# A two-layer decoder trunk: the four weight-block sums of each seven-product pair are issued on GpSimd instead of VectorE

## The chip, the cores and the metric

The kernel runs on one core of a Trainium2 chip. The metric is the device time of one execution in microseconds (us), as a median over runs. In the profile's rows PE is TensorE's matmuls and PEld its weight loads, DVE is VectorE, ACT is ScalarE, POOL is GpSimd, and SPq is the queue of SyncE, which here only issues transfers.

## The reference

The trunk has two layers on 512 tokens of width 1024. Each layer runs a feed-forward block, a token mixer (latent attention in layer 0, sparse attention with shared keys and values in layer 1, each with four memory heads beside it) and a second feed-forward block, each followed by a layer norm. Only the four feed-forward blocks matter here:

```python
def swiglu(x, w_gu, w_down):
    g, u = jnp.split(x @ w_gu, 2, axis=-1)
    return (jax.nn.silu(g) * u) @ w_down
x = layer_norm(DN_ALPHA * x + 0.5 * swiglu(x, ffn_w_gu[layer, 0], ffn_w_down[layer, 0]), ...)
```

Here `w_gu` is 1024 x 5632, so each block has 22 column blocks of 128 for g and 22 for u, and `w_down` is 2816 x 1024.

## The kernel before, in words

**Precision.** Every operand is kept as two fp32r tiles, a rounded part `hi` and a remainder `lo`, and a product is three matmuls: hi·hi, hi·lo, lo·hi. Weights are read from HBM as f32 tiles of 128 x 1024 (`wraw`, a pool of 5 buffers, loaded on SP's queue by `load`, line 143). `split` makes the two parts: ScalarE casts the raw tile to `whi` (L216), VectorE writes `wlo` = raw − hi (L217), which has two inputs in SBUF. A pair `whi`, `wlo` lives in a ring of three, with four more inside the feed-forward blocks; it comes free when TensorE has read it for the last time.

**Seven products instead of eight.** In a feed-forward block, column block m of g and of u is computed for two halves of the tokens (columns 0 to 255 and 256 to 511), and the contraction over 1024 rows is cut in two halves of 512. That is a 2 x 2 by 2 x 2 product of blocks, and for 77 of the 88 column blocks (items "d" of the table `GROUPS`) it is done with seven block products. They need sums of token blocks, made once for each feed-forward block (`token_forms`, L427), and four sums of weight blocks for each pair (`combined`), with raw tiles g and u and a third one, d:

- L159: d(upper half) = g(lower) − u(lower)
- L160: u(lower) = u(lower) + u(upper)
- L165: d(lower) = u(lower) − g(lower)
- L168: g(upper) = g(upper) − d(lower)

Each is 128 x 512 f32 with both inputs in SBUF, and each reads what one before it wrote. The weight units of a pair are g0 (the raw g), g2 (the tile d), g1 (the tile u) and g3 (the upper half of g). `prep` makes unit after unit in the order of a list (`_unit_order`), up to four units ahead of the one that TensorE is to use.

**One pair on TensorE.** `sevens` runs for each pair j the products p6 and p7 (with d), the first half of the next pair (`m1`, with its g0), p5 and p4 (with u), the second half `m2` of the next pair, and p3 (with g3). Each of the seven is a `quarter`: 12 matmuls of 256 columns into half a PSUM bank. Between them stand short steps of other engines on PSUM banks: ScalarE copies a started bank into a new one (`seeded`, L590) and p7's result to SBUF (L613), VectorE adds p5's result to it (L618) and p4's (L622), both with one input in PSUM, and ScalarE applies silu (L603, L627). p5 accumulates into bank r2, L618 reads r2, and p3 accumulates on into the same r2: so p3 can start only when L618 has read the bank. Between p5 and p3 TensorE has p4 and `m2`. `finish` (L631, then a split to `hhi`, `hlo`) makes the input of the down projection.

**Groups.** The 22 column blocks are done in five groups of four or five. After each group the down projection adds its part for all four token tiles (L449 to L454, six matmuls of 512 columns each), and VectorE adds the result to the residual (L341, one input in PSUM). The first group of a block begins with two or three column blocks without the seven products (L643, L644).

**What sets the order.** The instructions of each engine run in the order in which the scheduler of the tile framework put them; each waits by semaphores for its inputs and buffers, and everything behind a waiting instruction on its engine waits too. The sums stand in VectorE's queue between the remainders of weight tiles (L217) and the steps on PSUM banks. GpSimd has, in the feed-forward blocks, two small transfers at the start (`apart`, L723) and four scalar powers in the norm at the end (L354); its other work lies in the attention.

Of the kernel before, what the change touches and what calls it, by code (L numbers as in the profile page):

```python
# [117 lines left out]
def tile_trunk(ctx: ExitStack, tc, a: dict, out):  # L118
    nc = tc.nc
# [21 lines left out]
    def load(src, n=1024):  # L141
        raw = wraw.tile([P, 1024], F32, name="wraw")
        nc.sync.dma_start(raw[:, :n], src[:, :n])
        return raw

    def combined(name, idx):


        l, f, m = idx
        lo, up = slice(0, 512), slice(512, 1024)  # L150
        op = nc.vector.tensor_tensor
        if name == "g0":
            W.pairs[idx] = [load(a["gu"][l, f, m, 0])]
            return W.pairs[idx][0]
        raws = W.pairs[idx]
        if len(raws) == 1:
            g, u, d = raws[0], load(a["gu"][l, f, m, 1]), wraw.tile([P, 1024], F32, name="wraw")
            raws += [u, d]
            op(d[:, up], g[:, lo], u[:, lo], op=ALU.subtract)  # L159
            op(u[:, lo], u[:, lo], u[:, up], op=ALU.add)  # L160
        g, u, d = raws
        if name == "g1":
            return u
        if name == "g2":
            op(d[:, lo], u[:, lo], g[:, lo], op=ALU.subtract)  # L165
            return d
        del W.pairs[idx]
        op(g[:, up], g[:, up], d[:, lo], op=ALU.subtract)  # L168
        return g[:, up]
# [9 lines left out]
    def prep():  # L179
        name, idx, n, scope = order[W.done]  # L180
        if name in ("g0", "g1", "g2", "g3"):
            raw = combined(name, idx)
            n = 512 if name == "g3" else n
        else:
            src = a[name]
            for i in idx:
                src = src[i]
            raw = load(src, n)
        hi, lo = ring(scope)
        split(hi[:, :n], lo[:, :n], raw[:, :n])  # L190
        W.ready[W.done] = (hi, lo)
        W.done += 1
# [1506 lines left out]
```

## Time and profile before

| | |
|---|---|
| time, median of 3 runs | 1850.78 us (1848.37 to 1850.85) |
| time of the profiled execution | 1853.04 us |
| its span | 1851.3 us |
| granted TensorE clock | 0.996 |

The profiled execution is 2.26 us above the median, and 1.74 us of its time lie outside the span. In the rows below, a group of instructions has its line, engine, operation and tiles (out <- in) with sizes in partitions x elements, then the count, the busy time in us and the mean of one in ns, then the idle time of the engine just before these instructions and what ended it. In a timeline the first column is the start in us, the second the duration in us; "x2" marks neighbours that were merged.

### The profile page before, as it was taken

The numbers are of one execution on the slowest core, as the hardware profiler recorded it, in microseconds if no ns is written. First come the engines' busy times: TensorE is split into PE (matmuls) and PEld (weight loads), VectorE is DVE, ScalarE is ACT, GpSimd is POOL, SyncE is SP. The second block draws the span as 40 slices with busy tenths as digits, with TensorE's granted clock in tenths as the row PEclk, the third lists the DMA queues.
The fourth block names the chain that finished last, engine by engine and source line by source line (L and its number), as shares of the span: only waits on it lengthen the run. The fifth ranks groups of instructions, "written<-read, shape, count | busy, mean of one in ns | idle before, by whom it ended". The sixth has DMA issues, their size and how long they took to land.

```text
span 1851.3 us, 31666 instructions
## 1 busy us (share of the span) xinstructions
PE 1831.2 (99%) x12753; PEld 1650.7 (89%) x12753; DVE 1346.2 (73%) x1979; ACT 914.9 (49%) x1671; POOL 170.3 (9%) x216
## 2 busy tenths in 40 slices
PE   9999999999999999999999999999999999999998
PEld 8899899996789999999999999999956699999997
DVE  8677777758678678677886876877667477677776
ACT  6345445456545345345653543544476354534542
POOL 0000000125500000000100000001266100000000
PEclk9999999999999999999999999999999999999999
DMA  7333235531134234224333323335321323323421
GB/s 259 103 126 111 97 112 162 181 107 35 58 112 156 70 102 149 69 92 160 123 120 115 125 83 112 115 121 171 107 56 21 124 71 120 114 82 112 132 75 69
DMA packets 60900, 204.90 MB, mean 111 GB/s; under 512 B 7152, under 2 KB 8320, under 8 KB 60752
## 3 DMA queue, kind: packets, MB, share of 16 engines
q1 hardware_dynamic: 57568, 194.46, 32.0%
q0 software_dynamic: 2752, 8.01, 1.3%
q8 instruction: 100, 1.64, 0.4%
q14 instruction: 48, 0.39, 0.1%
q10 hardware_dynamic: 432, 0.39, 0.1%
HBM read 188.16 MB, written 7.34 MB: 106 GB/s over the span
## 4 chain that ended last, share of the span: by engine, by line
PE 92%; DVE 4%; ACT 2%; issue 1%; DMA 1%; POOL 1%; POOLq 0%; DVEq 0%; ACTq 0%
PE bank L411 13%; PE bank L413 13%; PE bank L417 13%; PE bank L450 5%; PE bank L449 5%; PE bank L452 5%; PE bank L451 5%; PE bank L453 5%; PE bank L454 5%; PE bank L399 3%; PE bank L397 3%; PE bank L402 3%; PE tb L799 3%; PE o L827 2%; PE bank L386 2%; PE bank L384 2%
## 5 line engine op out<-in xcount | busy, mean ns | idle before, releaser
L216 ACT CAST whi<-wraw 128x1024 fp32r<-128x1024 f32 (+2 forms) x475 | 460.4, 977 | 534.2 <-PE bank L454 263.2
L217 DVE TENSOR_TENSOR wlo<-wraw,whi 128x1024 fp32r<-128x1024 f32 (+2 forms) x475 | 533.4, 1133 | 200.0 <-ACT whi L216 192.8
L411 PE MATMUL bank<-t,whi 128*128 128x256 f32 x1212 | 291.9, 277 | 0.0
L413 PE MATMUL bank<-t,whi 128*128 128x256 f32 x1212 | 291.6, 277 | 0.0
L413 PEld LDWEIGHTS bank<-t,whi 128*128 128x128 f32 x1212 | 227.8, 188 | 0.6
L411 PEld LDWEIGHTS bank<-t,whi 128*128 128x128 f32 x1212 | 227.7, 188 | 0.7
L411 PE MATMUL bank<-xhi,whi 128*128 128x256 f32 x924 | 223.0, 278 | 0.1
L413 PE MATMUL bank<-xlo,whi 128*128 128x256 f32 x924 | 222.2, 277 | 0.0
L417 PE MATMUL bank<-t,wlo 128*128 128x256 f32 x1232 | 190.6, 277 | 0.0
L411 PEld LDWEIGHTS bank<-xhi,whi 128*128 128x128 f32 x924 | 173.6, 188 | 2.4 <-DVE us L618 0.9
L413 PEld LDWEIGHTS bank<-xlo,whi 128*128 128x128 f32 x924 | 173.7, 188 | 1.2
L417 PEld LDWEIGHTS bank<-t,wlo 128*128 128x128 f32 x1232 | 163.3, 188 | 0.0
L341 DVE SCALAR_TENSOR_TENSOR x<-x,bank 128x512 f32<-128x512 f32 x176 | 112.2, 683 | 53.9 <-PE bank L453 51.7
L417 PE MATMUL bank<-xhi,wlo 128*128 128x256 f32 x924 | 143.1, 277 | 0.0
L354 POOL TENSOR_TENSOR st<-st,cst 128x1 f32<-128x1 f32 x24 | 15.8, 659 | 1368.0 <-DVE st L353 1343.1
L449 PE MATMUL bank<-whi,hhi 128*128 128x512 f32 x336 | 131.0, 390 | 0.0
L450 PE MATMUL bank<-whi,hhi 128*128 128x512 f32 x336 | 130.9, 390 | 0.0
L451 PE MATMUL bank<-wlo,hhi 128*128 128x512 f32 x336 | 130.8, 389 | 0.0
L454 PE MATMUL bank<-whi,hlo 128*128 128x512 f32 x336 | 130.7, 389 | 0.0
L452 PE MATMUL bank<-wlo,hhi 128*128 128x512 f32 x336 | 130.7, 389 | 0.0
L453 PE MATMUL bank<-whi,hlo 128*128 128x512 f32 x336 | 130.7, 389 | 0.0
L399 PE MATMUL bank<-xlo,whi 128*128 128x256 f32 x520 | 125.2, 281 | 2.3 <-DVE xlo L217 2.3
(340 smaller groups left out, 3592.1 us busy)
## 6 DMA issues: line engine op xcount, KB each, us to landing
wraw<-in_gu SPq DMA_DIRECT2D x173, 512.0 KB, 3.8
wraw<-in_dn SPq DMA_DIRECT2D x88, 512.0 KB, 4.1
wraw<-in_wo SPq DMA_DIRECT2D x16, 512.0 KB, 3.4
wraw<-in_wm SPq DMA_DIRECT2D x8, 512.0 KB, 4.3
x_dram<-x SPq DMA_DIRECT2D x8, 512.0 KB, 3.0
x<-x_dram SPq DMA_DIRECT2D x8, 512.0 KB, 4.4
wraw<-in_w SPq DMA_DIRECT2D x8, 512.0 KB, 3.4
wraw<-in_wq SPq DMA_DIRECT2D x6, 512.0 KB, 4.3
```

The costliest lines, as they stand in the source:

```text
L216: nc.scalar.copy(hi, src)
L217: return eng.tensor_tensor(lo, src, hi.bitcast(F32), op=ALU.subtract).ins
L399: nc.tensor.matmul(ps[:, c0:c1], lhsT=hi[:, k * P:(k + 1) * P], rhs=F.xlo[:, k, c0:c1], start=False, stop=False)
L411: nc.tensor.matmul(ps, lhsT=hi[:, ks], rhs=(xh if k else fh)[:, k], start=start and k == 0, stop=False, skip_group_check=True)
L413: nc.tensor.matmul(ps, lhsT=hi[:, ks], rhs=(xl if k else fl)[:, k], start=False, stop=False, skip_group_check=True)
L417: nc.tensor.matmul(ps, lhsT=lo[:, ks], rhs=xh[:, k], start=False, stop=k == 3, skip_group_check=True)
L449: nc.tensor.matmul(p0, lhsT=ahi, rhs=hi[:, 0:512], start=first, stop=False)
L450: nc.tensor.matmul(p1, lhsT=ahi, rhs=hi[:, 512:1024], start=first, stop=False)
L451: nc.tensor.matmul(p0, lhsT=ahi, rhs=lo[:, 0:512], start=False, stop=False)
L452: nc.tensor.matmul(p1, lhsT=ahi, rhs=lo[:, 512:1024], start=False, stop=False)
L453: nc.tensor.matmul(p0, lhsT=alo, rhs=hi[:, 0:512], start=False, stop=last)
L454: nc.tensor.matmul(p1, lhsT=alo, rhs=hi[:, 512:1024], start=False, stop=last)
```

## The change

The four sums of each pair are issued on GpSimd. Nothing else in the source changes; tiles, buffers and the list of units are the same.

```diff
@@ combined
         lo, up = slice(0, 512), slice(512, 1024)
-        op = nc.vector.tensor_tensor
+        op = nc.gpsimd.tensor_tensor
```

308 instructions (4 in each of 77 pairs) leave VectorE's queue and enter GpSimd's. TensorE's and SyncE's queues stay as they were. On the two others, some neighbours change places too, because the scheduler reckons with other ends.

The first place is a pair in the middle of a group of the first feed-forward block: sums into tile `wraw_3384`, between the L622 of one pair and the L618 of the next. VectorE before:

```order
L622 TENSOR_TENSOR us_3117<-us_3117,bank_3154 128x256
L217 TENSOR_TENSOR wlo_3298<-wraw_3295,whi_3297 128x1024
L217 TENSOR_TENSOR wlo_3264<-wraw_3259,whi_3263 128x1024
L159 TENSOR_TENSOR wraw_3384<-wraw_3295,wraw_3382 128x512
L631 SCALAR_TENSOR_TENSOR sg_3168<-sg_3168,us_3117 128x512
L217 TENSOR_TENSOR wlo_3317<-wraw_3257,whi_3316 128x1024
L217 TENSOR_TENSOR hlo_3116<-sg_3168,hhi_3115 128x512
L217 TENSOR_TENSOR wlo_3362<-wraw_3170,whi_3361 128x512
L160 TENSOR_TENSOR wraw_3382<-wraw_3382 128x512
L165 TENSOR_TENSOR wraw_3384<-wraw_3382,wraw_3295 128x512
L168 TENSOR_TENSOR wraw_3295<-wraw_3295,wraw_3384 128x512
L618 TENSOR_TENSOR us_3256<-us_3256,bank_3189 128x256
```

VectorE now, at the same place:

```order
L622 TENSOR_TENSOR us_3117<-us_3117,bank_3154 128x256
L217 TENSOR_TENSOR wlo_3298<-wraw_3295,whi_3297 128x1024
L217 TENSOR_TENSOR wlo_3264<-wraw_3259,whi_3263 128x1024
L217 TENSOR_TENSOR wlo_3317<-wraw_3257,whi_3316 128x1024
L631 SCALAR_TENSOR_TENSOR sg_3168<-sg_3168,us_3117 128x512
L217 TENSOR_TENSOR wlo_3362<-wraw_3170,whi_3361 128x512
L217 TENSOR_TENSOR hlo_3116<-sg_3168,hhi_3115 128x512
L618 TENSOR_TENSOR us_3256<-us_3256,bank_3189 128x256
```

The four sums are gone from the row; between `wlo_3264` and L618 stand four instructions, all with two inputs in SBUF, and `wlo_3362` has changed places with `hlo_3116`.

The second place is GpSimd's queue in the first feed-forward block, from the transfers `apart` on. Before:

```order
L723 DMA apart_218<-t_560 128x256
L723 DMA apart_218<-t_561 128x256
L354 ISA
L354 TENSOR_TENSOR st_3621<-st_3621,cst_73 128x1
L354 TENSOR_TENSOR st_3660<-st_3660,cst_73 128x1
```

[...]

```order
L723 DMA apart_218<-t_560 128x256
L723 DMA apart_218<-t_561 128x256
L159 ISA
L159 TENSOR_TENSOR wraw_580<-wraw_572,wraw_578 128x512
L160 TENSOR_TENSOR wraw_578<-wraw_578 128x512
L165 TENSOR_TENSOR wraw_580<-wraw_578,wraw_572 128x512
L168 TENSOR_TENSOR wraw_572<-wraw_572,wraw_580 128x512
L159 TENSOR_TENSOR wraw_621<-wraw_588,wraw_619 128x512
```

[...]

The third place is ScalarE's queue in the same stretch. Before, the seed copy into `bank_616` stood ahead of the cast of the second pair's tile d (`wraw_621`):

```order
L643 ACTIVATE sg_564<-bank_225 128x512
L216 CAST hhi_219<-sg_564 128x512
L590 COPY bank_616<-bank_603 128x256
L216 CAST whi_625<-wraw_621 128x1024
L613 COPY us_571<-bank_629 128x256
```

Now:

```order
L643 ACTIVATE sg_564<-bank_225 128x512
L216 CAST whi_599<-wraw_572 128x512
L216 CAST whi_625<-wraw_621 128x1024
L216 CAST hhi_219<-sg_564 128x512
L590 COPY bank_616<-bank_603 128x256
```

The cast that waits for the second pair's third sum moved ahead of that copy.

## Prediction

> **What bounds the kernel now.** I read the page's busy times first, then the four stretches of the feed-forward blocks in a table by windows, then TensorE's own waits.
>
> ```profile
> span 1851.3 us, 31666 instructions
> PE 1831.2 (99%) x12753; PEld 1650.7 (89%) x12753; DVE 1346.2 (73%) x1979; ACT 914.9 (49%) x1671; POOL 170.3 (9%) x216
> ```
>
> The four windows 42 to 323, 583 to 863, 966 to 1253 and 1540 to 1820 us hold nearly all pairs; the last row of that table is their sum:
>
> ```profile
> sum 1128.00, PE 1127.88 PEld 1058.96 DVE 827.84 ACT 524.15 POOL 0.00; mean PE 281.97 PEld 264.74 DVE 206.96 ACT 131.04 POOL 0.00
> ```
>
> TensorE is busy in 1127.88 of 1128 us there; VectorE in 827.84 (73%); GpSimd in none. The longest of TensorE's waits over the whole span are these:
>
> ```profile
> PE tb L799 <- POOL pp L1401: 2.4, 2, 2.2
> PE bank L399 <- DVE xlo L217: 2.3, 1, 2.3
> PE bank L384 <- ACT hT L216: 2.2, 1, 2.2
> ```
>
> They lie in an attention, after a norm and in the shared keys, where no sum runs. So TensorE's own work bounds every stretch with sums, and its queue does not change. VectorE's load can be lightened without any gain; time can only be lost, where TensorE comes to wait for something that the change makes late.
>
> **The change part by part.** The sums, and the instructions beside them in VectorE's queue:
>
> ```profile
> L217 DVE TENSOR_TENSOR wlo<-wraw,whi 128x1024 fp32r<-128x1024 f32 x387 | 471.6, 1228 | 174.6 <-ACT whi L216 167.7 <-PE bank L399 0.8
> L159 DVE TENSOR_TENSOR wraw<-wraw 128x512 f32<-128x512 f32 x77 | 53.2, 691 | 16.1 <-DMA wraw<-in_gu 14.4
> L168 DVE TENSOR_TENSOR wraw<-wraw 128x512 f32<-128x512 f32 x77 | 53.1, 690 | 1.8
> L165 DVE TENSOR_TENSOR wraw<-wraw 128x512 f32<-128x512 f32 x77 | 53.0, 689 | 1.6
> L160 DVE TENSOR_TENSOR wraw<-wraw 128x512 f32<-128x512 f32 x77 | 52.9, 687 | 0.7
> ```
>
> Removed from VectorE: 53.2 + 53.1 + 53.0 + 52.9 = 212.2 us. Since TensorE waits for none of it, this is worth nothing by itself: the cover is the units made ahead, and it stays.
>
> Added to GpSimd: the trace has no sum there, but the same form, a subtraction of 128 x 512 f32 with both inputs in SBUF, ten times in the first attention:
>
> ```profile
> L217 POOL TENSOR_TENSOR qt<-f,qt 128x512 fp32r<-128x512 f32 x10 | 12.9, 1287 | 3.4 <-ACT qt L216 3.4
> ```
>
> 308 x 1.287 = 396 us, in stretches where GpSimd was idle. A chain of four takes 5.1 us, against 2.8 on VectorE. The delay of 2.3 us alone would be hidden, because VectorE's queue already spreads the chain: the worked pair below needs 5.7 us for it. [...]
>
> The real cost is that the two engines do not run such instructions side by side. From the timelines of GpSimd and VectorE in the first attention:
>
> ```profile
> 435.79 1.28 POOL L217 TENSOR_TENSOR qt<-f,qt 128x512 fp32r<-128x512 f32 x1
> 457.79 2.81 POOL L1078 TENSOR_TENSOR pp<-pp,rs 128x384 f32<-128x384 f32 x2 [0.83 <-DVE rs L1075]
> ```
>
> ```profile
> 436.02 2.14 DVE L217 TENSOR_TENSOR wlo<-wraw,whi 128x1024 fp32r<-128x1024 f32 x1
> 458.36 1.34 DVE L217 TENSOR_TENSOR wlo<-wraw,whi 128x1024 fp32r<-128x1024 f32 x1
> ```
>
> The first `wlo` began 0.23 us into GpSimd's instruction and took 2.14 us instead of 1.23: it ended 1.09 us after GpSimd did (438.16 against 437.07), so it stood still until then. In the second pair of rows VectorE went in between GpSimd's two instructions, and the second of these ended only at 460.60, 0.90 us after `wlo` (459.70). So whoever asks first has SBUF, the other stands, and they take turns. A turn costs 0.14 us less than the instruction's duration (1.09 of 1.23): 1.15 for a sum, 1.09 for a `wlo`, 0.55 for VectorE's forms of 512.
>
> What this does to a pair in the middle of a group, by VectorE's timeline, with TensorE's rows around it:
>
> ```profile
> 294.63 2.36 DVE L217 TENSOR_TENSOR wlo<-wraw,whi 128x1024 fp32r<-128x1024 f32 x2 [0.56 <-ACT whi L216]
> 297.03 0.69 DVE L159 TENSOR_TENSOR wraw<-wraw 128x512 f32<-128x512 f32 x1
> 297.64 0.68 DVE L631 SCALAR_TENSOR_TENSOR sg<-sg,us 128x512 f32<-128x512 f32 x1
> 298.24 1.22 DVE L217 TENSOR_TENSOR wlo<-wraw,whi 128x1024 fp32r<-128x1024 f32 x1
> 299.38 0.68 DVE L217 TENSOR_TENSOR hlo<-sg,hhi 128x512 fp32r<-128x512 f32 x1
> 299.98 0.68 DVE L217 TENSOR_TENSOR wlo<-wraw,whi 128x512 fp32r<-128x512 f32 x1
> 302.03 0.69 DVE L168 TENSOR_TENSOR wraw<-wraw 128x512 f32<-128x512 f32 x1
> 302.63 0.41 DVE L618 TENSOR_TENSOR us<-us,bank 128x256 f32<-128x256 f32 x1
> ```
>
> ```profile
> 301.27 0.50 PE L417 MATMUL bank<-t,wlo 128*128 128x256 f32 x3
> 304.33 0.28 PE L411 MATMUL bank<-xhi,whi 128*128 128x256 f32 x1
> ```
>
> p5 ends at 301.77, L618 could run from then and ran at 302.63, behind L168, and p3 begins at 304.33. L618 may start as late as 304.33 − 0.41 − about 0.05 for the signal = 303.87 before TensorE stands still. Now the sums' start: u's transfer was issued at 292.45 and takes 3.8 us.
>
> ```profile
> 292.45 0.33 SPq L143 DMA_DIRECT2D wraw<-in_gu  x1
> wraw<-in_gu SPq DMA_DIRECT2D x173, 512.0 KB, 3.8
> ```
>
> So L159 asks at 296.3, while VectorE is in its second `wlo` until 296.99, and from there they alternate in the new order: L159 to 298.14, `wlo` to 299.23, L160 to 300.38, L631 to 300.93, L165 to 302.08, the `wlo` of 512 to 302.63, L168 to 303.78, `hlo` to 304.33, and only then L618: about 0.5 us past the limit. If VectorE kept SBUF for its whole row, L618 would be in time and the loss nothing; if GpSimd did its four at full length first (5.15) with VectorE's 2.74 behind, L618 starts at 304.9, and 1.0 us is lost. I take 0.5, the alternation that the second pair of rows shows.
>
> How often? Before, L618 was the one waiting for TensorE in 29 of 77:
>
> ```profile
> L618 DVE TENSOR_TENSOR us<-us,bank x77: 410/415/423, 49.8 to 1818.7; 128x256 f32<-128x256 f32 x77
>   PE bank L417: 22.5, 29
> ```
>
> In the other 48 VectorE's queue was behind. By SP's issues plus 3.8 us, in about 20 of these all four sums fall between the L622 before and this L618, with u landing 5.5 to 6.9 us ahead of p5's end. The worked pair, at 5.5, is the tightest; at 6.9 nothing is lost. In the rest two or three sums fall ahead, or the pair is the first of its group and VectorE has had time. The mean is then 0.25, and 20 x 0.25 = 5 us. The bounds: 0, and 48 x 0.5 = 24.
>
> The weights themselves keep their cover. ScalarE's casts waited mostly for TensorE to free the ring and hardly for sums:
>
> ```profile
> ACT whi L216 <- PE bank L454: 263.2, 78, 10.5
> ACT whi L216 <- DVE wraw L165: 15.8, 9, 3.9
> ```
>
> A weight that waits for its buffer is early by the depth of the ring, so a sum late by 2 us reaches no matmul.
>
> The opening has less cover. GpSimd is free for the first sum at 29.81 (29.26 + 0.55), and now the second pair's cast of d stands ahead of the seed copy L590, which ran here, while p6, which writes the seeded bank, began at 44.18:
>
> ```profile
> 29.26 0.55 POOL L723 DMA_DIRECT2D apart<-t  x1 [0.56 <-DVE t L217]
> 331.74 0.56 POOL L354 TENSOR_TENSOR st<-st,cst 128x1 f32<-128x1 f32 x1 [301.93 <-DVE st L353]
> ```
>
> ```profile
> 42.99 0.36 ACT L590 COPY bank<-bank 128x256 f32<-128x256 f32 x1
> 44.18 0.28 PE L411 MATMUL bank<-t,whi 128*128 128x256 f32 x1
> ```
>
> Seven sums lie ahead of that cast (8.1 us at 1.15), alternating with four `wlo` and two forms of 512 (5.5): 29.8 + 13.6 = 43.4, then the cast (1.06), `hhi` (0.62) and the copy (0.36): 45.4, 1 us after p6 should begin. Bounds 0 and 3 (if each turn costs full durations); I take 1.
>
> The sum: 5 + 1 = 6 us on the profiled execution's 1853.04, 1859.0. It stands 2.26 above the median, so against that: 1856.8. That is +0.32%; about 0.2% (3.7 us) is what a measurement of this kernel can tell from no change.
>
> **The rivals.**
>
> *Hidden after all* (the other side: not slower). VectorE gets SBUF as often as it asks, or asks earlier, since 212 us of its own work are gone; then L618 keeps within its 2.1 us (301.77 to 303.87). For it: the worked pair misses the limit by only 0.5. Against it: in the rows at 458 VectorE and GpSimd took turns. It decides at one turn: one sum fewer ahead of L618 and nothing is lost. Time 1850.8, with up to 2 us more from the opening.
>
> [...]
>
> *SBUF turns bind everywhere.* Per pair VectorE's three `wlo` of 1024, one of 512, L631 and `hlo` need 3 x 1.09 + 3 x 0.55 = 4.9 us, the four sums 4.6: 9.5 us, while TensorE's seven products take about 9.0 (p4 and `m2`, two of them, from 301.77 to 304.33). If handing over costs more than I read, all 48 late pairs lose 0.5: 24 us, 1874.8. Against it: over the windows, the down projection leaves room, 615.6 + 396 = 1012 of 1128 us.
>
> *Faster.* TensorE's waits leave nothing to gain where the sums stand. I give 0.04 to this, 0.03 of it to a gain over 0.2% that no row shows.
>
> **How the numbers follow.** Likeliest, the turns of the worked pair plus the opening: 0.43, at 1856.8 (1853 to 1861). Hidden: 0.33. Reload: 0.09. Bound everywhere: 0.11. Faster: 0.04. Slower by over 0.2%: of the first about five sixths (0.36), and both the reload and the bound case, 0.56. Within 0.2%: the hidden case, the rest of the first, and 0.01 of the last: 0.41. Faster by over 0.2%: 0.03. The range takes in hidden and likeliest whole, the reload on top, and part of the way to the bound case: 1849.5 to 1868; above lie most of 0.11, below little.
>
> **What would show it.** In the profile after: VectorE about 212 us of own work less, but `wlo` with a mean well above 1228 ns, as it stands in turns; GpSimd's sums at 1.29 us and longer; TensorE's waits with L618 and `bank` L411 (p3 begins with it) in the middle of groups, some 5 us in all; the L590 copy after 44 us in the opening. [...] Wrong: no stretched `wlo`, or stretched ones and TensorE without a gap; or gaps that end with a cast (L216), which would mean that the cover of the ring is gone.

## The result and the profile after

The changed kernel took 1866.45 us (median of 4 runs, 1864.83 to 1869.51), the kernel before on the same chip 1850.24 (4 runs, 1848.37 to 1850.85). The ratio is 1.0091, with a 95% interval of 1.0074 to 1.0109: 16.2 us slower. The forecast was 6 us slower. The profiled execution after took 1864.83 us, 11.8 us more than the profiled one before.

The page's span and busy times:

```profile
span 1863.0 us, 31998 instructions
PE 1832.6 (98%) x12753; PEld 1651.8 (89%) x12753; DVE 1315.5 (71%) x1671; ACT 915.8 (49%) x1671; POOL 684.9 (37%) x524
```

VectorE lost 308 instructions, but only 30.7 us of busy time (1346.2 before): what was taken off came back as standing time in the rest. Four of its groups by form, all with two inputs in SBUF except the last, which reads one from PSUM:

```profile
L217 DVE TENSOR_TENSOR wlo<-wraw,whi 128x1024 fp32r<-128x1024 f32 x387 | 522.0, 1362 | 197.4 <-ACT whi L216 189.1 <-DMA wraw<-in_gu 0.6
L217 DVE TENSOR_TENSOR hlo<-sg,hhi 128x512 fp32r<-128x512 f32 x88 | 100.3, 1139 | 18.4 <-ACT hhi L216 17.2
L631 DVE SCALAR_TENSOR_TENSOR sg<-sg,us 128x512 f32<-128x512 f32 x77 | 84.4, 1096 | 1.4 <-ACT sg L627 1.4
L341 DVE SCALAR_TENSOR_TENSOR x<-x,bank 128x512 f32<-128x512 f32 x176 | 113.7, 684 | 80.0 <-PE bank L453 75.3 <-DMA wraw<-in_gu 1.2 <-PE bank L386 1.1
```

`wlo` went from 1228 to 1362 ns in the mean; `hlo` and L631 now take 1139 and 1096 for a form that takes 690 undisturbed; L341 stayed at 684. None of that says yet what it costs. TensorE's waits do:

```profile
PE bank L411 <- ACT bank L590: 8.9, 4, 3.0
PE bank L411 <- DVE us L618: 2.6, 1, 2.6
...
PE bank L384 <- ACT hT L216: 0.6, 1, 0.6
```

Four waits for the seed copy L590, one for L618: five places, not dozens. TensorE's 12,753 matmuls stand in the same order in both kernels, so the start of each after, less its start before, is what has been lost up to there. That difference goes up by 4.7 us at 46 us, 1.9 at 595, 2.2 at 975 and 4.2 at 1553: the openings of the four feed-forward blocks, 13.0 us (each to within some 0.3, by where one starts to count). It goes up by 3.9 at 203 us, in the middle of the first block, and by 0.6 or less at any pair elsewhere. It goes down by 4.0 around 940 us, in the shared keys, where no sum runs. There the profiled execution of before waited longer for `hT` (2.2 us instead of 0.6, up to 935.03), and behind that wait, from 934.8 to 942 us, TensorE's clock was at about half (0.54 and 0.51), by a table by windows of before (the column after the engines' busy times is the granted TensorE clock):

```profile
934.80:938.50 3.70, 3.47 (x16) 3.48 (x17) 3.50 (x7) 1.72 (x5) 0.00 (x0) 0.54 0.39 146
938.50:942.00 3.50, 3.50 (x18) 3.16 (x17) 1.24 (x3) 1.14 (x4) 0.00 (x0) 0.51 0.00 0
```

In the changed kernel it stayed at 1.00 there (942.8 to 950 us). I put that down to the executions and not to the change.

The first opening, by the timelines of GpSimd, ScalarE and TensorE after:

```profile
40.11 2.15 POOL L160 TENSOR_TENSOR wraw<-wraw 128x512 f32<-128x512 f32 x1
42.34 1.59 POOL L165 TENSOR_TENSOR wraw<-wraw 128x512 f32<-128x512 f32 x1
```

```profile
43.97 1.04 ACT L216 CAST whi<-wraw 128x1024 fp32r<-128x1024 f32 x1 [4.73 <-POOL wraw L165]
44.92 0.61 ACT L216 CAST hhi<-sg 128x512 fp32r<-128x512 f32 x1
45.44 0.36 ACT L590 COPY bank<-bank 128x256 f32<-128x256 f32 x1
```

```profile
45.85 0.42 PE L411 MATMUL bank<-t,whi 128*128 128x256 f32 x1 [3.05 <-ACT bank L590]
```

The copy is queued behind the cast that waits for the second pair's L165, as forecast, and TensorE stood 3.05 us. The matmul that follows takes 0.42 us instead of 0.28. In a table by windows of the same kernel:

```profile
40.00:45.80 5.80, 2.81 (x25) 2.60 (x23) 4.17 (x4) 1.83 (x4) 5.04 (x4) 1.00 0.53 164
45.80:49.50 3.70, 3.65 (x18) 3.65 (x19) 2.99 (x4) 2.22 (x5) 0.00 (x0) 0.54 0.57 173
49.50:60.00 10.50, 10.50 (x93) 10.50 (x93) 6.35 (x7) 6.20 (x10) 0.19 (x1) 1.00 0.57 201
```

In the 3.7 us behind the wait the clock was at 0.54, and 18 matmuls ran where some 33 fit at full clock (an estimate from the 93 in the next 10.5 us). So a wait of 3.05 us cost 4.7.

The fourth opening has no cast that waits for a sum in front of the copy. There it is VectorE and ScalarE in a row:

```profile
1547.86 1.18 DVE L217 TENSOR_TENSOR wlo<-wraw,whi 128x512 fp32r<-128x512 f32 x1
1548.96 1.79 DVE L217 TENSOR_TENSOR hlo<-sg,hhi 128x512 fp32r<-128x512 f32 x1
1550.68 1.21 DVE L217 TENSOR_TENSOR wlo<-wraw,whi 128x1024 fp32r<-128x1024 f32 x1
1551.81 0.67 DVE L644 SCALAR_TENSOR_TENSOR sg<-sg,bank 128x512 f32<-128x512 f32 x1
```

```profile
1552.52 0.62 ACT L216 CAST hhi<-sg 128x512 fp32r<-128x512 f32 x1 [0.59 <-DVE sg L644]
1553.04 0.37 ACT L590 COPY bank<-bank 128x256 f32<-128x256 f32 x1
```

The remainders ahead of L644 are lengthened by turns (1.18 and 1.79 instead of 0.69), L644 makes `sg` late, `hhi` waits for it, and L590 stands behind `hhi`. The second opening is of the same kind; in the third, casts wait for the first pair's L165.

### The profile page after: what moved, and what is told of

Its sections match the earlier page's. It is cut to its first block, busy times and chain, and to the rows that moved or that the text cites. A ratio compares the mean times of both kernels' runs of the same rounds, so it can differ in the third digit from the quotient of the medians.

```text
span 1863.0 us, 31998 instructions
## 1 busy us (share of the span) xinstructions
PE 1832.6 (98%) x12753; PEld 1651.8 (89%) x12753; DVE 1315.5 (71%) x1671; ACT 915.8 (49%) x1671; POOL 684.9 (37%) x524
## 5 line engine op out<-in xcount | busy, mean ns | idle before, releaser
L217 DVE TENSOR_TENSOR wlo<-wraw,whi 128x1024 fp32r<-128x1024 f32 (+2 forms) x475 | 620.3, 1319 | 228.7 <-ACT whi L216 219.3
L159 POOL TENSOR_TENSOR wraw<-wraw 128x512 f32<-128x512 f32 x77 | 132.2, 1717 | 530.3 <-DMA wraw<-in_gu 196.5
L413 PE MATMUL bank<-xlo,whi 128*128 128x256 f32 x924 | 224.0, 279 | 0.0
L341 DVE SCALAR_TENSOR_TENSOR x<-x,bank 128x512 f32<-128x512 f32 x176 | 113.7, 684 | 80.0 <-PE bank L453 75.3
L168 POOL TENSOR_TENSOR wraw<-wraw 128x512 f32<-128x512 f32 x77 | 121.7, 1580 | 110.0 <-issue 64.9
L160 POOL TENSOR_TENSOR wraw<-wraw 128x512 f32<-128x512 f32 x77 | 130.7, 1697 | 6.0
L165 POOL TENSOR_TENSOR wraw<-wraw 128x512 f32<-128x512 f32 x77 | 130.3, 1693 | 6.0
L451 PE MATMUL bank<-wlo,hhi 128*128 128x512 f32 x336 | 130.8, 389 | 0.0
L454 PE MATMUL bank<-whi,hlo 128*128 128x512 f32 x336 | 130.7, 389 | 0.0
```

Source lines behind the costliest of these rows:

```text
L217: return eng.tensor_tensor(lo, src, hi.bitcast(F32), op=ALU.subtract).ins
L413: nc.tensor.matmul(ps, lhsT=hi[:, ks], rhs=(xl if k else fl)[:, k], start=False, stop=False, skip_group_check=True)
L451: nc.tensor.matmul(p0, lhsT=ahi, rhs=lo[:, 0:512], start=False, stop=False)
L454: nc.tensor.matmul(p1, lhsT=alo, rhs=hi[:, 512:1024], start=False, stop=last)
```

## The experiments

Each time stands beside the kernel before, run on the same chip in the same set: 1849.4 us in the first set, 1850.46 in the second, 1850.41 in the third.

### Where the loss is: the first groups alone, and all but them

```diff
-        op = nc.gpsimd.tensor_tensor
+        op = (nc.vector if m < 5 else nc.gpsimd).tensor_tensor
```

> The sums of the first group's pairs of each feed-forward block (2, 2, 3 and 2 pairs, 36 sums) go back to VectorE; the other 272 sums stay on GpSimd. Theory A, the openings: of what TensorE lost in the changed kernel against the kernel before, matmul by matmul, 13.0 us arose at the seed copy L590 of the four openings and 3.9 us at one pair near 203 us; so the 13.0 go and 3.9 stay: about 1854 us (1850 to 1856), and no wait of TensorE ends with L590. Rival B, the turns on SBUF everywhere: 68 of 77 pairs keep their sums on GpSimd, so 68/77 of the 16.2 us stay, 14.3: about 1864.5 us.

The counterpart has the two engines exchanged:

```diff
-        op = nc.gpsimd.tensor_tensor
+        op = (nc.gpsimd if m < 5 else nc.vector).tensor_tensor
```

> The counterpart: only the 36 sums of the first group's pairs of each block go to GpSimd, the other 272 are on VectorE as in the kernel before. Theory A, the openings: nearly the whole loss is there: 1850.2 + 13 = about 1863 us, with waits of TensorE for L590 of 8 to 9 us in sum. Rival B, turns everywhere: 9/77 of 16.2 us, 1.9: about 1852 us.

Measured: with the first groups on VectorE 1853.94 us, a ratio of 1.0028 (1.0018 to 1.0039), by which 5.2 us are lost; with only the first groups on GpSimd 1860.55, 1.0060 (1.0047 to 1.0073), 11.1 us, somewhat less than the 13 expected. The two add up to 16.3 (15.7 by the medians), the whole loss within the noise. So 36 of the 308 sums cause two thirds of it; by the count of pairs it would be 1.9 us. TensorE's waits, of the first kernel and of the second:

```profile
PE bank L411 <- DVE us L618: 2.6, 1, 2.6
```

```profile
PE bank L411 <- ACT bank L590: 8.2, 4, 3.4
...
PE bank L411 <- DVE us L618: 0.4, 1, 0.4
```

Rival B, a loss spread over all pairs, is out.

### What makes the copy late at the openings

All sums stay on GpSimd; only the place of instructions around ScalarE's copy is changed. First the second pair's cast is held behind the copy:

```diff
-                nc.scalar.copy(r, src)
+                F.seed = nc.scalar.copy(r, src).ins
...
-                    ws = unit("g2", (l, f, m0 + j), 4)
+                    with tc.issue_after(F.seed) if n == 0 and gi == 0 else ExitStack():
+                        ws = unit("g2", (l, f, m0 + j), 4)
```

> All 308 sums on GpSimd, but ScalarE's queue mended: in each opening the cast of the second pair's d is held behind the first pair's seed copy L590. Theory A1, the cast ahead of the copy is what makes it late, as at 43.97 us in the first block: if in all four blocks, the 13.0 us go, about 1854 us. Theory A2: only the first block has that cast ahead of the copy; in the second and fourth the copy stands behind hhi, which waits for VectorE's L644, late behind remainders that took turns with sums, and in the third behind the first pair's own cast, which waits for its L165; then only the 4.7 us of the first block go: about 1861.7 us, with waits for L590 of some 6 us left. Rival B, turns everywhere: no change, 1866.4 us.

Measured: 1857.65 us, 1.0048 (1.0036 to 1.0060). Neither number I had written down: the loss is about half. Waits for L590 are still there (3.5 us, three times), and the first opening shows why, by ScalarE's timeline of this kernel:

```profile
43.61 0.62 ACT L216 CAST hhi<-sg 128x512 fp32r<-128x512 f32 x1 [4.19 <-DVE sg L644]
44.13 0.37 ACT L590 COPY bank<-bank 128x256 f32<-128x256 f32 x1
```

Without the cast the copy is only 1.3 us earlier (44.13 instead of 45.44), because `hhi` ahead of it is late in the same way as in the fourth block. I had seen the first cause there and missed the second, which lay right behind it. So next both go behind the copy: the last ordinary column block's split of `sg` is put off until the copy is issued (`F.seed` is the copy, as above; `items0` is the group's whole list of items).

```diff
-                split(hhi[:, j, :], hlo[:, j, :], sg)
+                if gi == 0 and j == items0.count("s") - 1:
+                    F.rest = hhi[:, j, :], hlo[:, j, :], sg
+                else:
+                    split(hhi[:, j, :], hlo[:, j, :], sg)
...
                     if n == 0 and gi == 0:
                         m1(j)
+                        with tc.issue_after(F.seed):
+                            split(*F.rest)
+                            ws = unit("g2", (l, f, m0 + j), 4)
```

> All 308 sums on GpSimd. In each opening the seed copy L590 is now ahead of both the second pair's cast of d and the last ordinary column block's hhi cast (whose input L644 stands on VectorE behind remainders that take turns with sums); those two come behind it. Theory A3, the copy's place in ScalarE's queue behind work that the sums delay is the whole cause at the openings: no wait of TensorE for L590 is left, only the 3.9 us of the pair near 203 us stay, as in the kernel with the first group on VectorE: about 1854 us. Rival: the copy, or the first pair's own weights, are late in themselves because the first pair's sums are: the 1857.65 us of the kernel with only the cast moved would hardly fall, 1857 us, and the waits would end with L216 or L590 as before.

Measured: 1854.13 us, 1.0023 (1.0015 to 1.0032), as theory A3 has it. No wait for L590 above 0.2 us is left. ScalarE's timeline of the same place:

```profile
41.39 0.36 ACT L590 COPY bank<-bank 128x256 f32<-128x256 f32 x1 [2.13 <-PE bank L588]
43.47 0.62 ACT L216 CAST hhi<-sg 128x512 fp32r<-128x512 f32 x1 [1.72 <-DVE sg L644]
```

The copy waits for TensorE alone; `hhi` is as late as before, and nobody needs it.

### The one place at 203 us

VectorE's timeline of the changed kernel, up to the L618 that came 4.94 us after p5's end, and TensorE's p3 behind it:

```profile
196.73 1.78 DVE L217 TENSOR_TENSOR hlo<-sg,hhi 128x512 fp32r<-128x512 f32 x1
198.44 2.31 DVE L217 TENSOR_TENSOR wlo<-wraw,whi 128x1024 fp32r<-128x1024 f32 x1
200.67 2.28 DVE L217 TENSOR_TENSOR mlo<-mr,mhi 128x1024 fp32r<-128x1024 f32 x1
202.87 0.41 DVE L618 TENSOR_TENSOR us<-us,bank 128x256 f32<-128x256 f32 x1
```

```profile
203.33 0.58 PE L411 MATMUL bank<-xhi,whi 128*128 128x256 f32 x1 [2.63 <-DVE us L618]
```

Three instructions each gave one turn to a sum (1.78, 2.31, 2.28 instead of 0.69, 1.22, 1.22). Elsewhere there are as many turns, but only here does VectorE also have the memory's remainder `mlo` ahead of L618. In the kernel before, this place already had no spare time: its L618 ended at 197.72 us, and p3 began 0.06 us later. To test it I first gave the sums of the pair to VectorE whose L618 is late (the last of the third group), once on top of the kernel with the first groups on VectorE and once on top of the one with the copy ahead of all:

```diff
-        op = nc.gpsimd.tensor_tensor
+        op = (nc.vector if m < 5 or idx == (0, 0, 13) else nc.gpsimd).tensor_tensor
```

```diff
-        op = nc.gpsimd.tensor_tensor
+        op = (nc.vector if idx == (0, 0, 13) else nc.gpsimd).tensor_tensor
```

> As the kernel with the first group's sums on VectorE, and in the first block the last pair of the third group (the one near 203 us, where VectorE also has the memory's remainders in its queue) on VectorE too: 40 sums there, 268 on GpSimd. Theory A, two places and nothing else: the last 3.9 us go, so the time is that of the kernel before, 1849.4 within 1.5 us, and 212.2 x 268/308 = 185 us off VectorE gain nothing. Rival B, a steady loss from turns: 3 us or more stay, 1852.5 us or above.

> The copy ahead of all, as in the first kernel of this set, with the one pair near 203 us on VectorE (4 sums there, 304 on GpSimd). If both causes are whole: as the kernel before, 1849.4 within 1.5 us; a gain of over 2 us is not expected, since TensorE has nothing to gain from VectorE. If the openings keep a loss of their own: 1853 us or more.

Measured: 1854.39 us, 1.0027 (1.0019 to 1.0036), and 1852.83, 1.0016 (1.0007 to 1.0026). Both miss the forecast of no difference. TensorE's timeline of the first shows the wait unchanged:

```profile
198.83 0.39 PE L411 MATMUL bank<-xhi,whi 128*128 128x256 f32 x1 [2.58 <-DVE us L618]
```

It was the wrong pair: the sums that run ahead of this L618 are those of the next pair (the first of the fourth group), made ahead as all weights are. With that pair's sums on VectorE instead:

```diff
-        op = nc.gpsimd.tensor_tensor
+        op = (nc.vector if m < 5 or idx == (0, 0, 14) else nc.gpsimd).tensor_tensor
```

```diff
-        op = nc.gpsimd.tensor_tensor
+        op = (nc.vector if idx == (0, 0, 14) else nc.gpsimd).tensor_tensor
```

> The first group's sums on VectorE, and those of the pair behind the one near 203 us: the L618 that is late there belongs to the last pair of the first block's third group, but the sums that take turns with the six instructions ahead of it are those of the next pair, the first of the fourth group. 40 sums on VectorE, 268 on GpSimd. Theory A, openings and this one place: the wait for L618 near 200 us goes, and the time is that of the kernel before within 1.5 us. Rival B, a steady loss from turns: 3 us or more stay.

> The copy ahead of all in the openings, and the sums of that same next pair on VectorE: 304 sums on GpSimd, 4 on VectorE. If the causes are whole: the kernel before within 1.5 us, no gain beyond that, since TensorE's work is the bound; the kernel with only the copy moved took 1854.1. Rival: 2.5 us or more stay.

Measured: 1850.70 us, 1.0003 (0.9994 to 1.0012), and 1850.53, 1.0002 (0.9993 to 1.0011). No loss that these runs can tell is left, with 268 and with 304 sums on GpSimd. Two groups of the second kernel, the remainders on VectorE and the first sum on GpSimd:

```profile
L217 DVE TENSOR_TENSOR wlo<-wraw,whi 128x1024 fp32r<-128x1024 f32 x387 | 519.0, 1354 | 185.8 <-ACT whi L216 177.6
```

```profile
L159 POOL TENSOR_TENSOR wraw<-wraw 128x512 f32<-128x512 f32 x76 | 131.8, 1734 | 530.0 <-DMA wraw<-in_gu 223.4 <-DVE wlo L217 204.7 <-DVE sg L631 54.2
```

The turns are all still there (1354 ns against 1228, a sum 1734 instead of about 1290), and they cost nothing. Nor is there a gain: VectorE's own work is lighter by 304 sums, and no time is won, because TensorE has nothing to wait for. No version beat the kernel before.

### How near the other pairs are: one more turn

The first groups are on VectorE; in the other 68 pairs GpSimd does L159 twice, the same result written again.

```diff
             op(d[:, up], g[:, lo], u[:, lo], op=ALU.subtract)
+            if m >= 5:
+                op(d[:, up], g[:, lo], u[:, lo], op=ALU.subtract)
```

> As the kernel with the first group's sums on VectorE, but in the other 68 pairs GpSimd does the first sum L159 twice (the same result, written again): one more turn on SBUF for each pair. Theory C, the turns decide at one turn: in the changed kernel L618 ended less than 1.15 us ahead of p3 in 38 of 77 pairs (mostly 0.48 to 0.63 us ahead); if each of these is held back by one more turn of 1.15 us, the sum of what they overrun is about 24 us, so some 20 us more than the kernel with the first group on VectorE: about 1875 us, with TensorE's waits for L618 of 10 us or more. Rival D, VectorE is not held back by GpSimd where it matters: the second L159 only lengthens GpSimd's chain, and the time is that of the kernel without it, within 2 us.

Measured: 1869.52 us, 1.0110 (1.0097 to 1.0124), 15.6 us more than the kernel without the second L159 (1853.94). TensorE's waits (L620 is the L618 of this file, two lines down), the second row those of the weight loads:

```profile
PE bank L413 <- DVE us L620: 8.5, 12, 2.7
```

```profile
PEld bank L413 <- DVE us L620: 13.5, 15, 3.1
```

L618 waits for none of the sums. It is late because its engine gave one turn more, so the turns themselves are shown to hold VectorE back, and the spare time of these pairs is less than one turn. Theory C holds in kind and not in size. Matmul by matmul against the profiled execution without the second L159, 7.8 of 14.4 us arise at 13 starts of p3 right behind this L618, where it had expected all 38. The rest arises elsewhere (2.0 us of it between 1300 and 1400 us, where no sum runs), and its cause stays open.

A variant puts a GpSimd copy (one input in SBUF) in place of the second L159:

```diff
+            if m >= 5:
+                nc.gpsimd.tensor_copy(d[:, up], u[:, lo])
             op(d[:, up], g[:, lo], u[:, lo], op=ALU.subtract)
```

> The first group's sums on VectorE; in the other 68 pairs GpSimd writes the upper half of d once more ahead of L159, with a copy of the lower half of u (one input in SBUF instead of two; L159 overwrites it). Compared with the kernel that does L159 twice there (1869.5 us, L618 waited for 12 times, 8.5 us): if an instruction with one input holds VectorE back as one with two, about 1869 us again, and VectorE's remainders as long; if only two inputs on both sides do, the copy costs GpSimd's chain its own time and no turn: between 1854 and 1858 us.

Measured: 1855.93 us, 1.0029 (1.0017 to 1.0041), as the kernel without the copy (1.0028). The time is the one I gave for "no turn", but the rows say otherwise. GpSimd's timeline and VectorE's:

```profile
118.44 0.61 POOL L160 COPY wraw<-wraw 128x512 f32<-128x512 f32 x1 [8.42 <-DVE wlo L219]
```

```profile
118.51 1.62 DVE L219 TENSOR_TENSOR wlo<-wraw,whi 128x1024 fp32r<-128x1024 f32 x1
```

The `wlo` that began 0.07 us into the copy took 1.62 instead of 1.22. So a copy takes its turn too, only a short one, of 0.4 us here, which the spare time still covers. The expectation's reasoning ("only two inputs on both sides do") is wrong.

### What a wait of TensorE costs beyond itself

The kernel before, without any sum on GpSimd, with extra copies of the bank ahead of L618, which overwrites their result:

```diff
             with tc.high_priority():
+                for _ in range(4 + F.dose % 8):
+                    nc.vector.tensor_copy(us[j][:, c1], r2[j])
                 op(us[j][:, c1], us[j][:, c0], r2[j], op=ALU.add)
```

> The kernel before, with 4 to 11 extra copies of the same PSUM bank on VectorE ahead of L618 (their result is overwritten by L618); the number goes round over the 77 pairs, GpSimd has no sums. It makes TensorE wait for L618 by 0 to some 3 us at 77 places. Theory E, the clock gate: in the changed kernel matmuls ran at 213 instead of 113 ns from start to start for about 3.4 us after the waits of 2.36, 2.63 and 3.05 us, and not after those of 1.36 and 2.10; so here waits over about 2.2 us are followed by such a stretch and cost some 1.5 us beyond themselves, and shorter ones are not. Rival F, the slow stretch comes with GpSimd's work and not with the wait: no slow stretch here after any wait. [...]

It took 1886.38 us (one run), but its waits reached only 1.8 us, so the second set of doses has `8 + F.dose % 11`:

> As the kernel before with extra copies ahead of L618, now 8 to 18 of them, so that TensorE waits 0.5 to 4 us at 77 places. Theory E, as far as the first doses bore it out: waits of up to 1.4 us are never followed by a stretch at half clock, those between about 1.8 and 3 us sometimes, by where they fall, the longer ones always or nearly; each stretch has some 16 matmuls of 256 columns at 213 ns from start to start instead of 113, 1.6 us. [...]

It took 1963.24 us (one run). One of its waits, of 3.44 us, ended at 678.65; the windows behind it:

```profile
678.60:682.50 3.90, 3.85 (x20) 3.71 (x21) 3.60 (x6) 1.69 (x3) 0.00 (x0) 0.64 0.20 53
682.50:690.00 7.50, 7.50 (x65) 7.50 (x65) 6.30 (x10) 5.35 (x11) 0.00 (x0) 0.96 0.64 218
```

GpSimd does nothing here and the clock falls all the same, to 0.64 in the 3.9 us behind the wait, so rival F is out. All waits of TensorE of over 0.7 us ahead of p3 and p6 in the feed-forward blocks (for L618 or L590, one of them for a cast), from the traces of the changed kernel and of the experiments, by whether the matmuls of the 8 us behind them lost 1.4 us or more from start to start (113 ns is usual for 256 columns, 213 in a slow stretch):

| wait of TensorE | waits | with a slow stretch |
|---|---|---|
| 0.71 to 1.71 us | 25 | 0 |
| 1.82 to 2.72 us | 15 | 10 |
| 2.97 to 4.14 us | 9 | 9 |

A stretch cost 1.4 to 1.8 us in 18 of 19 cases (2.2 in one). Waits of the same length fall on both sides in the middle row (2.10 us with and without), so length alone does not decide; whether it depends on where a wait falls is not shown. Theory E holds, but without the sharp limit of 2.2 us that the first expectation gave it. The limits of this table hold for these places alone: in the shared keys a wait of 1.3 us (for `hT`, in the kernel with the copy ahead of all; TensorE had worked in only 1.94 of the 3.8 us up to its end) was followed by 3.5 us at a clock of 0.50, and the 2.2 us of before, above, by a clock of 0.54 and 0.51 in two windows of 7.2 us in all.

## Why the prediction was right in direction and short in size

**The bound, and nothing to gain: right.** With the five places mended, 268 or 304 sums off VectorE gave 1.0003 and 1.0002 times the time before.

**Price of a sum and of a turn: right.** In the opening the first sum, which had SBUF first, took 1.31 us (at 29.70 us; the forecast took 1.287); and where the engines take turns there, the rows follow the forecast of 1.15 us for a sum, 1.09 for a `wlo` and 0.55 for `hlo` to within 0.05.

```profile
29.04 0.55 POOL L723 DMA_DIRECT2D apart<-t  x1 [0.56 <-DVE t L217]
29.70 1.31 POOL L159 TENSOR_TENSOR wraw<-wraw 128x512 f32<-128x512 f32 x1
```

The reload to which the forecast gives 0.09 is a term that no run shows: in the same rows the first sum began 0.11 us behind the transfer, with its usual duration.

**The worked pair: the step that failed is when L159 may ask.** I let it ask when u had landed, inside the second `wlo`, and so go ahead of the third. It writes into d's buffer, which the second `wlo` must first have read. GpSimd and VectorE of the changed kernel at this pair:

```profile
304.06 2.37 POOL L159 TENSOR_TENSOR wraw<-wraw 128x512 f32<-128x512 f32 x1 [6.24 <-DVE wlo L217]
306.51 1.62 POOL L160 TENSOR_TENSOR wraw<-wraw 128x512 f32<-128x512 f32 x1
```

```profile
304.05 1.23 DVE L217 TENSOR_TENSOR wlo<-wraw,whi 128x1024 fp32r<-128x1024 f32 x1
305.19 1.78 DVE L631 SCALAR_TENSOR_TENSOR sg<-sg,us 128x512 f32<-128x512 f32 x1
306.90 1.78 DVE L217 TENSOR_TENSOR wlo<-wraw,whi 128x512 fp32r<-128x512 f32 x1
308.60 1.77 DVE L217 TENSOR_TENSOR hlo<-sg,hhi 128x512 fp32r<-128x512 f32 x1
310.30 0.41 DVE L618 TENSOR_TENSOR us<-us,bank 128x256 f32<-128x256 f32 x1
```

L159 asked 0.01 us after the third `wlo` had begun and got its turn only behind it. So three sums instead of four ran ahead of L618, which ended 0.63 us ahead of p3 instead of coming 0.5 us too late. That is the rival "hidden after all" with the very condition it named, one sum fewer. It holds for the pairs in general: in 38 of 77 L618 ended less than one turn (1.15) ahead of p3, mostly 0.48 to 0.63, and at all but a few of these TensorE did not stand.

**The steady term: about the size, at another place.** Forecast 5 us over some 20 pairs; measured 3.9 us at one pair, where `mlo` shares VectorE's queue, and next to nothing at the others. The mechanism was the one forecast; its spread was not. That the two sizes are near is chance.

**The opening: the term that was mis-sized.** The copy's end was forecast at 45.4 us and came at 45.80, so the delay itself was near. But I charged 1 us, once. It was 13.0, for four reasons. I took the time at which TensorE comes to p6 (44.18) from one execution. In the profiled execution after, it was ready 1.4 us earlier, at 42.80: its matmuls followed each other faster (90 of them between 20 and 30 us, 87 before). Of the 3.05 us that it stood, only 1.67 are later than 44.18. There are four openings, and I had looked at the first alone: my sum charges one. In the other three the sums reach L590 by another way, through `hhi` and L644, which I did not follow. And a wait of some 2 us or more can bring a slow stretch that costs 1.5 us, which I had no term for: in the changed kernel those of 3.05, 2.63 and 2.36 us at L590 and L618 did, and the one of 2.10 us at L590 did not.

**The weights' cover: right.** No wait of TensorE over 0.5 us in these blocks ended with a cast.

**The range.** The measured time lies inside 1849.5 to 1868 because the range reached part of the way to the case that turns bind everywhere. That case did not come about, so it is luck that the range took the time in.

What stays open: the four runs of the changed kernel spread over 4.7 us. Slow stretches that come or not would do that, as the one at 935 us came before and not after; it was not tested.

## What to carry to other kernels

Work moved off a loaded engine onto one that takes turns with it on SBUF does not leave that engine (of the 212.2 us of sums taken off VectorE, 30.7 us went from its busy time): look for the short steps queued there on which the bounding engine waits, count the turns ahead of each, and compare them with its spare time. Do this at every place where the pipeline starts anew, not only in the steady state and not only at the first, and follow two engines back from the step, since a late step can reach it through a queue that holds neither the moved work nor its reader. In these blocks a wait of TensorE of 1.82 to 2.72 us was followed by a slow stretch in 10 of 15 cases and one of 2.97 us or more in 9 of 9, at 1.4 to 1.8 us each in 18 of the 19; in work as dense, charge such waits about 1.5 us beyond themselves in that share of the cases, as an estimate from these counts.

## What the runs showed of the hardware

**Turns.** VectorE instructions with two inputs in SBUF and GpSimd's sums run one at a time: `hlo`, 0.69 us alone, took 1.77 when it stood behind a sum (308.60 us in the rows above). L341 and L618, with one input in PSUM, ran beside the sums undisturbed (684 and 414 ns on average, 683 and 417 before). In the changed kernel an L341 lies wholly inside a sum, by the timelines of VectorE and GpSimd, and neither took longer than alone:

```profile
151.40 0.69 DVE L341 SCALAR_TENSOR_TENSOR x<-x,bank 128x512 f32<-128x512 f32 x1 [0.19 <-PE bank L453]
```

```profile
151.35 1.29 POOL L159 TENSOR_TENSOR wraw<-wraw 128x512 f32<-128x512 f32 x1 [4.20 <-DVE wlo L217]
```

The one-input copy on GpSimd (0.61 us) held a `wlo` back by 0.4 us. That it is SBUF for which they take turns is inferred from which instructions stood and which did not; no row names it.

**The granted clock.** At p3 and p6, behind all 9 TensorE waits of 2.97 us and more the matmuls slowed down by 1.4 us or more over the next 8 us, behind 1.82 to 2.72 us in 10 of 15, and behind shorter ones in none of 25. The granted clock was 0.54 in the 3.7 us after the first opening's wait of 3.05 us, and 0.64 in the 3.9 us after the one of 3.44 us with the extra copies. In the shared keys it fell behind a shorter wait too (0.50 for 3.5 us behind 1.3 us), and for longer (0.54 and 0.51 in two windows of 7.2 us in all, behind 2.2 us). 1.82 us of waiting was enough in the blocks; how long a wait has to last, and why waits of one length fall on both sides, is not shown.
